# A whole first-stage order, row factors and pool scale by transposes, and 36 idle transposes at the start of TensorE

## Chip, cores and metric

One core of one Trainium2 chip runs the kernel. The metric is the device time of one execution in microseconds: 1158.05 us, the median of three runs (1158.02, 1158.05 and 1160.07). An instruction's place is given in us from the start of the profiled span.

## What is computed

Two layers over 512 latent rows and 256 context rows of 1024 channels. Layer 0 mixes by pooling, layer 1 by attention, and a squared-ReLU MLP follows each. The change touches the start of layer 0: row norm, conditioning vectors, the pooling mixer, and the first matmuls of its MLP. Cut to that:

```python
def modulate(h, shift, scale):
    return h * (1.0 + scale) + shift

def pool_mixer(h, w_pool, pool_scale):
    ...
        mean = (jnp.take(csg, hi, axis=1) - jnp.take(csg, lo, axis=1)) / cnt
        diff = (mean - hf[..., sl]).astype(h.dtype)
        outs.append(diff @ w_pool[g])
    return jnp.concatenate(outs, axis=-1) * pool_scale

def reference(...):
    for i in range(DEPTH):
        sh1, sc1, gt1, sh2, sc2, gt2 = ada_mods(c, w_ada[i], b_ada[i])
        csh1, csc1, cgt1, csh2, csc2, cgt2 = ada_mods(c_ctx, w_ada[i], b_ada[i])
        h_lat = modulate(rms_norm(x, g_mix_pre[i]), sh1, sc1)
        h_ctx = modulate(rms_norm(ctx, g_mix_pre[i]), csh1, csc1)
        ...
        x = x + gt1 * rms_norm(y_lat, g_mix_post[i])
        m_lat = sq_relu_mlp(modulate(rms_norm(x, g_mlp_pre[i]), sh2, sc2), w_mlp_in[i], w_mlp_out[i])
        x = x + gt2 * rms_norm(m_lat, g_mlp_post[i])
        ...
    return x
```

## The kernel before

Rows lie in six tiles of 128: t = 0 to 3 are latent, t = 4 and 5 context. The 1024 channels are eight blocks k of 128, two to each of the four pooling windows g. Large matmuls take operands split into a rounded half and a remainder (`hi` and `lo`), three products for one.

The first stage is written by hand. `FIRST` is one list of steps, and each step emits the instructions of one small piece of work. TensorE, VectorE and ScalarE keep the order in which the list emits their instructions (the wrapper `Kept`), and each executes them in that order; so a step that waits holds back all later steps of its engine, and no others. After the stage a scheduler places the instructions with a simulated timeline. Weight loads go through SyncE (SP) in program order, into seven raw buffers of 1 MB: four in `rawe`, three in `rawp`; `turns` says for each conditioning block which of the two pools it takes. A load is issued when its buffer is free.

The names of the steps:

- Row norm: `rows_a(t)` takes the mean square on ScalarE, adds epsilon on VectorE and takes the power on GpSimd; `rows_b(t)` (step `rb`) scales the row tile on VectorE into `acc`. Before the list, six `rows_a` and five `rows_b` stand at times of their own.
- Band: `band_mm(t, ks)` multiplies the scaled row tile by a band matrix (window mean minus identity), one fp32 matmul, which is two instructions, for each k; it writes `psm` (latent) or `psc` (context). `band_edge(v)` builds the bands of the first and the last tile from the loaded one. `ev` and `evc` move the sums to SBUF, on ScalarE where the step has a star, otherwise on VectorE.
- Conditioning: `mm:X_j` multiplies a loaded block of `w_ada` by the two conditioning vectors (the sums lie in 32-row groups), `rows` transposes it on VectorE, `sel` adds the groups by four small matmuls, `mods` adds the bias. SC1, SH1, GT1, SC2 and SH2 are the scale, shift and gate of the mixer and the scale and shift of the MLP. The blocks are loaded in the order SC1 and SH1 (0 to 3 in turn), GT1_0a, GT1_0b, GT1_2a, GT1_2b, `w_in`, SC2_0a, SC2_0b, SH2_0a, SH2_0b, SC2_2, SH2_2, SC2_3, SH2_3.
- Pooling: `wsc` multiplies the pool weights by `pool_scale`, which `pool_weights` spreads over the partitions by a matmul with one row; `wph` and `wpl` split them; `hi` and `lo` scale and split the band sums of a block k; `pool:t:g` makes six matmuls; `ms`, `rs` and `c` take its mean square, its factor and a copy.
- Gate and residual: `gc` makes gate columns, `psg` (`gate_half`) spreads four of them over the partitions by four fp32 matmuls against the identity, `gate` copies them to SBUF, `b` multiplies, `r` adds to `xr`.
- MLP input: `s`, `rs2` and `n` norm the new rows, `turn` transposes them (four transposes of 128x128), `h` modulates, `xhi` and `xlo` split, `in:t:q:f` makes six matmuls of the MLP; `whi` and `wlo` split its weights.

PSUM has two pools: `psA`, two buffers of two banks, and `psB`, four buffers of one bank. `psA` holds the latent band sums, the pool products of tiles 0, 2, 3 and 5 and the MLP sums; `psB` holds the rest.

Of the kernel before, what the change touches and what calls it, by code (L numbers as in the profile page):

```python
# [17 lines left out]
P = 128  # L18
# [13 lines left out]
HALO = 8  # L32
# [9 lines left out]
ev:0* ev:2 psc0:4 psm:4 rb:5 wsc:0 psm:6 wsc:1 ev:4* wph:0 mm:SC1_0 wph:1 wpl:0 mm:SH1_0 ev:6* rows:SC1_0 wpl:1  # L42
psc0:5 sel:SC1_0 rows:SH1_0 evc:2* mods:SC1_0 evc:0* sel:SH1_0 mm:SC1_1 mods:SH1_0 hi:0 psc:4 rows:SC1_1 hi:1
psc:6 lo:0 mm:SH1_1 evc:4* lo:1 evc:6* sel:SC1_1 rows:SH1_1 pool:4:0 mods:SC1_1 sel:SH1_1 mm:SC1_2 mods:SH1_1
hi:2 pool:0:0 rows:SC1_2 pool:5:0 hi:3 lo:2 mm:SH1_2 lo:3 sel:SC1_2 rows:SH1_2 pool:4:1 mods:SC1_2 sel:SH1_2
ms:4:0 mm:SC1_3 mods:SH1_2 hi:4 c:4:0 pool:5:1 rows:SC1_3 mm:SH1_3 hi:5 lo:4 sel:SC1_3 pool:0:1 rows:SH1_3
mods:SC1_3 sel:SH1_3 lo:5 pool:1:0 pool:1:1 mods:SH1_3 pool:5:2 hi:6 mm:GT1_0a ms:1:0 lo:6 pool:4:2 hi:7
mm:GT1_0b c:1:0 lo:7 pool:0:2 mm:GT1_2a rows:GT1_0 pool:4:3 sel:GT1_0 ms:4:1 mm:GT1_2b w_in mods:GT1_0 gc:0:0
gc:1:0 c:4:1* rs:4 pool:0:3 rows:GT1_2 psg:0:0 ms:0 sel:GT1_2 psg:1:0 c:0* mods:GT1_2 rs:0 gc:0:1 gc:1:1 psg:1:1
gate:1:0 gate:0:0 pool:5:3 b:4:0 gate:1:1 b:1:0 mm:SC2_0a ms:5 b:4:1 psg:0:1 r:4 c:5* rs:5 pool:1:2 gate:0:1 b:5  # L50
mm:SC2_0b s:4 pool:1:3 r:5 whi:0 rs2:4 pool:3:0 ms:1:1 rows:SC2_0 pool:3:1 c:1:1* b:0 mm:SH2_0a rs:1 n:4*
sel:SC2_0 b:1:1 mm:SH2_0b s:5 r:0 pool:2:0 whi:1 rs2:5 pool:2:1 rows:SH2_0 pool:2:2 s:0 mods:SC2_0 r:1 sel:SH2_0
mm:SC2_2 n:5* rs2:0 mods:SH2_0 wlo:0 pool:2:3 s:1 turn:4:0 n:0 turn:4:1 ms:2 rs2:1 mm:SH2_2 h:4:1 h:4:0* rs:2
pool:3:2 n:1 xhi:4:0 mm:SC2_3 rows:SH2_2 xhi:4:1 rows:SC2_2 xlo:4:0 sel:SH2_2 turn:0:1 xlo:4:1 sel:SC2_2 h:0:1*
pool:3:3 mods:SH2_2 mods:SC2_2 turn:0:0 b:2 xhi:0:1 mm:SH2_3 ms:3 xlo:0:1 in:4:0:1 h:0:0* rows:SH2_3 rs:3
in:4:1:1 b:3 xhi:0:0 in:0:1:1 r:3 turn:0:2 in:4:0:0 h:0:2* xlo:0:0 in:4:1:0 s:3 r:2 in:0:1:0 in:0:0:1 xhi:0:2
# [36 lines left out]
def backbone(ctx: ExitStack, tc, x, ctx_in, w_ada, w_pool, pool_scale, w_qkv, g_q, g_k, w_o, w_mlp_in,  # L93
# [134 lines left out]
    given = phase[:, 16:32]  # L228
    sy.dma_start(given, vecs[:, 160:176])
# [10 lines left out]
    one = sm_tile("sm")  # L240
    ve.memset(one, 1.0)
# [87 lines left out]
    def gate_half(ci, h):  # L329
        ps = psB.tile([P, 512], F32, tag="b", name="psg")  # L330
        gc = halfgate.pop((ci, h))
        for k in range(4):
            te.matmul(ps[:, k * P:(k + 1) * P], gc[:, 4 * h + k:4 * h + k + 1].broadcast_to([P, P]), ident,
                      start=True, stop=True)
        halfgate[ci, h] = ps
# [105 lines left out]
    def band_edge(v):  # L441
        c = (HALO, P)[v]
        ve.tensor_copy(bands[:, v], bands[:, 2])
        ve.tensor_copy(bands[:, v, :, c:c + HALO], edges[:, v])

    band_edge(0)

    means, lat, con = {}, {}, {}

    def band_open(k):  # L450
        lat[k] = psA.tile([P, 2, 512], F32, tag="a", name="psm")
        for u in range(2):
            means[k + u] = lat[k][:, u, :], None

    def band_open_c(k):
        con[k] = psB.tile([P, 2, 256], F32, tag="b", name="psc")
        for u in range(2):
            means[k + u] = means[k + u][0], con[k][:, u, :]

    def band_mm(t, ks):  # L460
# [4 lines left out]
        for k in ks:  # L465
            te.matmul(means[k][q][:, lo:hi], accv[:, t, k * P:(k + 1) * P], bands[:, v, k // 2, c0:c0 + hi - lo],
                      start=(i == 0 and (q == 0 or k % 2 == 0)), stop=(i == n - 1), skip_group_check=True)

    def band_ev(k, q, on_act):
        to = accv[:, (0, NL)[q]:(NL, NT)[q], P * k:P * k + 256]  # L470
        (sc.copy if on_act else ve.tensor_copy)(to, (lat, con)[q][k].rearrange("p u (a n) -> p (u a) n", n=256))
        for u in range(2):
            means[k + u] = (means[k + u][0], to[:, u, :]) if q else (to[:, 2 * u:2 * u + 2, :], means[k + u][1])
# [3 lines left out]
    def rows_a(t):  # L477
        ss, ms, rs[t] = sm_tile("ss"), sm_tile("ms"), sm_tile("rs")
        mean_square(xr[:, t, :], ss[:, 0:1])
        ve.tensor_scalar(out=ms[:, 0:1], in0=ss[:, 0:1], scalar1=EPS, scalar2=None, op0=ALU.add)  # L480
        gp.tensor_tensor(out=rs[t][:, 0:1], in0=ms[:, 0:1], in1=nhalf[:, 0:1], op=ALU.pow)

    def rows_b(t):
        scaled(accv[:, t, :], t, rs[t])
# [16 lines left out]
    pw = []  # L501
# [22 lines left out]
    def pool_a(t, g):  # L524
        if t not in mix:
            if t in (4, 1):
                mix[t] = [psB.tile([P, 512], F32, tag="b", name="pspool") for _ in range(2)]
            else:
                mix[t] = psA.tile([P, 2, 512], F32, tag="a", name="pspool")
# [251 lines left out]
    turns.extend((0, 0, 0, 0, 1, 1, 0, 0, 1, 0, 0, 1, 0, 0, 1, 0, 0, 1, 0, 0))  # L781
# [15 lines left out]
    st.at(14, pool_load)
# [33 lines left out]
    def keep(store, key, fn, *args):  # L831
# [3 lines left out]
        rb=rows_b, psc0=lambda t: band_mm(t, range(4)), psm=band_rows, psc=band_context,  # L835
# [23 lines left out]
    for n, what in enumerate(FIRST.split()):  # L859
        st.at(14.5 + n / 1000, step, what)  # L860
# [671 lines left out]
_INS = ["x", "ctx", "w_ada", "w_pool", "pool_scale", "w_qkv", "g_q", "g_k", "w_o", "w_mlp_in", "w_mlp_out"]  # L1532
_VECS = ["b_ada", "g_mix_pre", "g_mlp_pre", "g_mix_post", "g_mlp_post", "c", "c_ctx"]
# [78 lines left out]
```

## Time and profile before

| | |
|---|---|
| median of the three runs | 1158.05 us |
| time of the profiled execution | 1160.61 us |
| its span, first to last instruction | 1158.8 us |
| mean granted TensorE clock | 0.999 |
| TensorE busy with matmuls | 99% of the span |
| VectorE, ScalarE, GpSimd busy | 81%, 55%, 6% |
| DMA, mean over the span | 127 GB/s |

A row of the timeline gives start, duration, engine, line, operation, output and inputs, and the count of instructions merged in it; brackets hold the idle time before it and what ended that. A row of the chain of waits gives start, duration, what the time belonged to, and a count. Steps emitted through the wrapper all carry line L89, so they are told apart by tile names: `psm` and `psc` band sums, `psada` conditioning, `pspool` pooling, `psg` spread columns, `psx` transposes, `psin` MLP input.

### The profile page before, as it was taken

To read this page: it belongs to the slowest core of one execution; us is meant where nothing else is said; L and a number is where in the kernel's file an instruction comes from. 1 tells how busy PE (TensorE), PEld (TensorE's weight loads), DVE (VectorE), ACT (ScalarE), POOL (GpSimd) and SP (SyncE) were. 2 spreads that over 40 slices of the span, in tenths; PEclk is the share of its full clock that TensorE was granted. 3 is DMA by queue.
4 is the path that set the end of the run, shared out by engine and by line. 5 is a ranking of instruction groups with operands and counts; after the bars stand their busy time and mean duration, and the time that the engine had idled before them with its cause. 6 is when DMAs were issued, how large, how long until landed. Compare 5 with 4: busy or idle time off the path is not lost.

```text
span 1158.8 us, 16048 instructions
## 1 busy us (share of the span) xinstructions
PE 1142.9 (99%) x6220; PEld 992.7 (86%) x6220; DVE 932.9 (81%) x1522; ACT 632.8 (55%) x1076; POOL 69.7 (6%) x113
## 2 busy tenths in 40 slices
PE   7999999999999999999999999999999999999997
PEld 5789899898898988998888889998988888888886
DVE  4699588889988997996777699867687679778876
ACT  5687555555354534555675367753676436534523
POOL 1050000000000000000242200001100000000001
PEclk9999999999999999999999999999999999999999
DMA  9973222334344444343522102115244214313212
GB/s 374 419 282 140 73 103 107 130 139 143 112 146 146 145 146 145 109 146 109 182 74 73 37 1 74 37 74 186 105 141 150 77 69 146 109 40 142 109 32 114
DMA packets 25518, 147.34 MB, mean 127 GB/s; under 512 B 2785, under 2 KB 5345, under 8 KB 9698
## 3 DMA queue, kind: packets, MB, share of 16 engines
q1 hardware_dynamic: 25442, 146.32, 34.8%
q8 instruction: 49, 0.80, 0.3%
q14 instruction: 27, 0.22, 0.1%
HBM read 138.96 MB, written 7.34 MB: 126 GB/s over the span
## 4 chain that ended last, share of the span: by engine, by line
PE 91%; issue 2%; DVE 2%; ACT 2%; POOL 2%; DMA 1%; SPq 0%; POOLq 0%; DVEq 0%; ACTq 0%
PE pso L890 24%; PE psin L745 18%; PE psin L621 16%; PE pso L1001 12%; PE psy L1427 3%; PE po L1402 3%; PE pss L1361 3%; PE psq L1147 2%; PE pspt L1383 2%; PE pspool L89 2%; PE psada L89 2%; PE psin L89 2%; PE psm L89 1%; PE psx L89 1%; PE psg L89 1%
## 5 line engine op out<-in xcount | busy, mean ns | idle before, releaser
L890 PE MATMUL pso<-units,rb 128*128 128x512 f32 x1152 | 278.5, 392 | 0.0
L890 PEld LDWEIGHTS pso<-units,rb 128*128 128x128 f32 x1152 | 214.8, 188 | 41.2
L304 DVE SCALAR_TENSOR_TENSOR rows<-raw,cond,rows 128x256 f32<-128x256 f32 x280 | 127.5, 480 | 2.0
L904 DVE TENSOR_TENSOR acc<-acc,pso 128x512 f32<-128x512 f32 x126 | 84.0, 682 | 40.8 <-PE pso L890 40.7
L621 PE MATMUL psin<-ra,rb 128*128 128x512 f32 (+1 forms) x310 | 87.8, 360 | 0.0
L1001 PE MATMUL pso<-units,pairs 128*128 128x512 f32 x336 | 82.6, 389 | 0.0
L621 PE MATMUL psin<-ra 128*128 128x512 f32 (+1 forms) x256 | 76.5, 376 | 0.0
L1001 PEld LDWEIGHTS pso<-units,pairs 128*128 128x128 f32 x336 | 63.1, 188 | 13.1
L1005 DVE TENSOR_TENSOR acc<-acc,pso 128x512 f32<-128x512 f32 x72 | 48.7, 683 | 26.3 <-PE pso L1001 26.3
L212 POOL TENSOR_SCALAR ms<-ss 128x1 f32<-128x1 f32 x15 | 10.4, 691 | 969.6 <-ACT junk L199 924.1
L745 PE MATMUL psin<-ra,units 128*128 128x384 f32 x336 | 65.6, 337 | 0.4 <-ACT psin L757 0.4
L745 PE MATMUL psin<-sums,units 128*128 128x384 f32 x336 | 64.1, 337 | 0.0
L745 PEld LDWEIGHTS psin<-ra,units 128*128 128x128 f32 x336 | 59.7, 188 | 4.0 <-ACT psin L757 0.9
L621 PEld LDWEIGHTS psin<-ra,rb 128*128 128x128 f32 x310 | 55.6, 189 | 8.7
L745 PEld LDWEIGHTS psin<-sums,units 128*128 128x128 f32 x336 | 58.9, 188 | 1.6
L171 DVE TENSOR_TENSOR units<-raw,units 128x1024 fp32r<-128x1024 f32 (+2 forms) x49 | 55.2, 1152 | 4.9 <-ACT units L168 4.8
L621 PE MATMUL psin<-rb 128*128 128x512 f32 (+1 forms) x155 | 55.8, 361 | 0.6 <-DVE rb L1496 0.6
L168 ACT CAST units<-raw 128x1024 fp32r<-128x1024 f32 (+2 forms) x49 | 46.8, 995 | 16.9 <-PE pso L890 12.8
L621 PEld LDWEIGHTS psin<-ra 128*128 128x128 f32 x256 | 47.1, 188 | 8.8
L902 ACT COPY acc<-pso 128x512 f32<-128x512 f32 x48 | 27.2, 588 | 48.7 <-PE pso L890 48.4
L1147 PE MATMUL psq<-units,ra 128*128 128x512 f32 x216 | 52.2, 393 | 0.0
L621 PE MATMUL psin<-rb,ra 128*128 128x512 f32 (+1 forms) x128 | 48.1, 376 | 0.0
(292 smaller groups left out, 2395.0 us busy)
## 6 DMA issues: line engine op xcount, KB each, us to landing
raw<-in_w_ada SPq DMA_DIRECT2D x48, 1024.0 KB, 5.1
raw<-in_w_mlp_in SPq DMA_DIRECT2D x32, 1024.0 KB, 4.9
raw<-in_w_mlp_out SPq DMA_DIRECT2D x32, 1024.0 KB, 5.0
raw<-in_w_qkv SPq DMA_DIRECT2D x6, 1024.0 KB, 5.0
spill<-xr SPq DMA_DIRECT2D x10, 512.0 KB, 5.5
xr<-spill SPq DMA_DIRECT2D x10, 512.0 KB, 7.0
raw<-in_w_o SPq DMA_DIRECT2D x4, 1024.0 KB, 4.9
xr<-in_x SPq DMA_DIRECT2D x4, 512.0 KB, 6.5
```

The source lines that it names most:

```text
L89: return lambda *args, **kw: self.tc.keep_in_program_order(f(*args, **kw))
L168: a = sc.copy(hi, raw)
L171: b = ve.tensor_tensor(out=lo, in0=raw, in1=hi, op=ALU.subtract)
L304: ve.scalar_tensor_tensor(out=r, in0=raw[:, k, :], scalar=cond[:, k, c:c + 1], in1=r, op0=ALU.mult, op1=ALU.add)
L621: te.matmul(ps[:, bank, o:o + ln], w[:, k, fs], rhs, start=start, stop=(k == KT - 1 and n == 2), skip_group_check=len(ks) < KT or self.paired)
L745: te.matmul(bank, w[k], a[k], start=start and k == 0 and m == 0, stop=stop and k == 3 and m == 2, skip_group_check=True)
L890: te.matmul(pss[h][:, 0:cols[h][1]], a[:, f, ts_], w[:, f, cols[h][0]:sum(cols[h])], start=(n == 0 and not seeded[t]), stop=(n == len(seq) ...
L904: ve.tensor_tensor(out=d, in0=d, in1=ps[:, 0:w], op=ALU.add)
L1001: te.matmul(ps, a, w, start=(m == 0), stop=(m == len(seq) - 1))
L1005: ve.tensor_tensor(out=M[n][:, t], in0=M[n][:, t], in1=ps, op=ALU.add)
L1147: te.matmul(ps, a[:, k, sl], w[:, k % 4, :], start=(k == 0 and n == 0), stop=(k == KT - 1 and n == 2))
L1361: te.matmul(ps[:, c2, 0:384], a[:, sl], b[:, kv, 384 * c2:384 * c2 + 384], start=(n == 0), stop=(n == 2))
```

## The change

The steps of the row norm, the band edges and all band matmuls become entries of `FIRST`, which starts at time 1 and holds the whole stage in a new order. The stars say where an evacuation, a norm or a modulation runs.

```diff
 FIRST = """
-ev:0* ev:2 psc0:4 psm:4 rb:5 wsc:0 psm:6 wsc:1 ev:4* wph:0 mm:SC1_0 wph:1 wpl:0 mm:SH1_0 ev:6* rows:SC1_0 wpl:1
-psc0:5 sel:SC1_0 rows:SH1_0 evc:2* mods:SC1_0 evc:0* sel:SH1_0 mm:SC1_1 mods:SH1_0 hi:0 psc:4 rows:SC1_1 hi:1
...
-rs2:3 wlo:1 s:2 in:0:0:0 turn:0:3 xlo:0:2 n:3* sel:SH2_3 rs2:2 turn:4:2 rows:SC2_3 in:0:2:0 mods:SH2_3 h:4:2*
...
+xs:0 xe:0 xp:0 xn:0 xs:1 xe:1 xs:2 edge:0 xp:1 psm:0:2 xn:1 xs:3 psm:0:0 xe:2 psm:0:4 xp:2 psm:1:2 xs:4 xn:2
+psm:1:4 psm:0:6 xe:3 xp:3 edge:1* psm:2:4 xe:4 psm:2:2 xp:4 xn:3 xs:5 psm:1:0 psm:3:4 psm:3:2 ev:4* xe:5 psm:2:0
+xp:5 xn:4* psm:3:0 pw:0 ev:5* psm:1:6 wsc:0 psm:2:6 psm:3:6 pw:1 ev:7* ev:6 wph:0 wsc:1 mm:SC1_0 ev:0* psc:4:0
+rows:SC1_0 xn:5 mm:SH1_0 wph:1 sel:SC1_0 ev:2* rows:SH1_0 psc:5:0 mods:SC1_0 psc:4:2 evc:0 sel:SH1_0 psc:5:2
+mods:SH1_0 mm:SC1_1 wpl:0 hi:0 psc:4:6 rows:SC1_1 evc:2* psc:5:6 lo:0 hi:1 mm:SH1_1 sel:SC1_1 evc:6* psc:4:4
+mods:SC1_1 psc:5:4 rows:SH1_1 lo:1 sel:SH1_1 evc:4* mm:SC1_2 mods:SH1_1 pool:0:0 rows:SC1_2 hi:2 wpl:1 pool:5:0
+hi:3 sel:SC1_2 mm:SH1_2 lo:2 pool:1:0 mods:SC1_2 rows:SH1_2 sel:SH1_2 mm:SC1_3 mods:SH1_2 lo:3 hi:4 pool:4:0
+pool:1:1 lo:4 mm:SH1_3 ms:1:0 rows:SC1_3 hi:5 pool:4:1 rows:SH1_3 c:1:0 sel:SC1_3 sel:SH1_3 pool:5:1 mods:SH1_3
+mods:SC1_3 pool:0:1 lo:5 hi:7 mm:GT1_0a hi:6 lo:7 pool:0:2 mm:GT1_0b ms:4:0 lo:6 pool:5:2 rows:GT1_0 pool:0:3
+c:4:0 sel:GT1_0 ms:0 mm:GT1_2a mods:GT1_0 gc:1:0 gc:0:0 psg:0:0 rs:0 c:0 pool:1:2 gate:0:0 mm:GT1_2b w_in
+psg:1:0 rows:GT1_2 pool:1:3 gate:1:0 b:1:0 sel:GT1_2 pool:2:0 whi:0 mods:GT1_2 gc:0:1 gc:1:1 b:4:0 psg:0:1
+ms:1:1 pool:5:3 wlo:0 gate:0:1 pool:4:2 rs:1 c:1:1* b:0 pool:4:3 ms:5 psg:1:1 b:1:1 pool:2:1 ms:4:1 rs:5 r:0
+mm:SC2_0a c:4:1* gate:1:1 rs:4 mm:SC2_0b r:1 c:5* pool:2:2 s:0 b:4:1 pool:3:0 r:4 s:1 pool:3:1 rs2:0 pool:3:2
+rows:SC2_0 s:4 rs2:1 pool:2:3 b:5 n:0* mm:SH2_0a rs2:4 n:1 mm:SH2_0b ms:2 r:5 sel:SC2_0 n:4* turn:0:1 rows:SH2_0
...
+xhi:4:0 mm:SH2_3 h:4:2* xlo:4:0 in:0:1:1 whi:1 rows:SH2_3 in:4:1:0 r:3 s:2 in:4:0:1 sel:SH2_3 in:4:0:0 s:3
...
+in:2:2:1 h:2:0* xlo:2:1 in:2:2:0 xhi:2:0 in:2:3:0 xlo:2:0 in:2:1:0 in:2:0:1 in:2:0:0 in:2:3:1 in:4:3:1 in:2:1:1
 """
```

The steps behind the new names: `xs`, `xe`, `xp` and `xn` are the three parts of `rows_a` and `rows_b`, with `xn` on ScalarE under a star; `psm:t:k` and `psc:t:k` are `band_mm` for one row tile and two blocks; the sums of blocks 4 to 7 go to four `psB` buffers in place of two `psA` buffers.

```diff
+    def awake(n):
+        ps = psB.tile([P, 512], F32, tag="b", name="idle")
+        for k in range(n):
+            te.transpose(ps[:, (k % 4) * P:(k % 4 + 1) * P], ident, ident)
...
-    turns.extend((0, 0, 0, 0, 1, 1, 0, 0, 1, 0, 0, 1, 0, 0, 1, 0, 0, 1, 0, 0))
+    turns.extend((0, 0, 0, 0, 1, 1, 0, 0, 0, 0, 1, 1, 0, 0, 0, 0, 1, 1, 0, 0))
...
-    st.at(0.1, pool_weights, 0)
...
-    st.at(14, pool_load)
+    st.at(0.05, awake, 36)
+    st.at(0.5, pool_load)
```

`pool_scale` is no longer loaded as a row; it comes with the vectors, as eight columns, and is spread by transposes, and so are the gate columns:

```diff
-    given = phase[:, 16:32]
-    sy.dma_start(given, vecs[:, 160:176])
+    given, pool_cols = phase[:, 16:32], phase[:, 32:40]
+    sy.dma_start(phase[:, 16:40], vecs[:, 160:184])
...
     xload(0)
-    scale_row = work_tile()[0:1]
-    sy.dma_start(scale_row, pool_scale[0:1])
+    xload(1)
     sy.dma_start(gate.rearrange("p a n -> p (a n)")[:, 8 * BW:12 * BW + 64], band)
-    for t in range(1, NT):
+    for t in range(2, NT):
         xload(t)
...
         for k in range(4):
-            te.matmul(ps[:, k * P:(k + 1) * P], gc[:, 4 * h + k:4 * h + k + 1].broadcast_to([P, P]), ident,
-                      start=True, stop=True)
+            te.transpose(ps[:, k * P:(k + 1) * P], gc[:, 4 * h + k:4 * h + k + 1].broadcast_to([P, P]), ident)
...
     def pool_weights(h):
         ps = psB.tile([P, 512], F32, tag="b", name="psg")
-        te.matmul(ps, one[0:1, 0:1].broadcast_to([1, P]), scale_row[:, 512 * h:512 * h + 512], start=True, stop=True)
-        pw.append(ps)
+        for k in range(4):
+            te.transpose(ps[:, k * P:(k + 1) * P], pool_cols[:, 4 * h + k:4 * h + k + 1].broadcast_to([P, P]), ident)
+        pooled_scale[h] = ps
```

The pool products of tiles 4 and 1 take their second `psB` buffer when the second half begins, where before they took both at once. `gate_half` is also called twice in layer 1.

More of the change, by code (lines that the diff above doesn't have):

```diff
@@ L47 @@
[L47 to L56, printed above, removed]
@@ new lines @@
+ms:1:1 pool:5:3 wlo:0 gate:0:1 pool:4:2 rs:1 c:1:1* b:0 pool:4:3 ms:5 psg:1:1 b:1:1 pool:2:1 ms:4:1 rs:5 r:0
+mm:SC2_0a c:4:1* gate:1:1 rs:4 mm:SC2_0b r:1 c:5* pool:2:2 s:0 b:4:1 pool:3:0 r:4 s:1 pool:3:1 rs2:0 pool:3:2
+rows:SC2_0 s:4 rs2:1 pool:2:3 b:5 n:0* mm:SH2_0a rs2:4 n:1 mm:SH2_0b ms:2 r:5 sel:SC2_0 n:4* turn:0:1 rows:SH2_0
+mm:SC2_2 s:5 mods:SC2_0 sel:SH2_0 rows:SC2_2 pool:3:3 mods:SH2_0 rs2:5 b:2 h:0:1* turn:0:0 sel:SC2_2 mm:SH2_2
+h:0:0* n:5 mods:SC2_2 turn:4:0 xhi:0:0 rows:SH2_2 turn:4:1 ms:3 xlo:0:0 sel:SH2_2 mm:SC2_3 mods:SH2_2 xhi:0:1
@@ new lines @@
+rs:3 b:3 in:0:0:0 h:4:1* turn:4:2 rs:2 xlo:0:1 xhi:4:1 in:0:0:1 rows:SC2_3 h:4:0* in:0:1:0 xlo:4:1 r:2 sel:SC2_3
+xhi:4:0 mm:SH2_3 h:4:2* xlo:4:0 in:0:1:1 whi:1 rows:SH2_3 in:4:1:0 r:3 s:2 in:4:0:1 sel:SH2_3 in:4:0:0 s:3
+mods:SH2_3 rs2:2 mods:SC2_3 wlo:1 turn:0:2 xhi:4:2 turn:4:3 rs2:3 in:4:1:1 h:4:3* xlo:4:2 turn:0:3 n:2 h:0:2*
+in:4:2:0 n:3 in:4:2:1 xhi:4:3 turn:2:3 xhi:0:2 xlo:4:3 turn:2:1 h:0:3* turn:2:2 xlo:0:2 in:4:3:0 h:2:1 xhi:0:3
+in:0:2:1 h:2:2* xlo:0:3 in:0:2:0 h:2:3 xhi:2:2 in:0:3:1 xlo:2:2 in:0:3:0 xhi:2:3 xhi:2:1 turn:2:0 xlo:2:3
@@ L92, in backbone @@
 @with_exitstack
[L93 removed]
+def backbone(ctx: ExitStack, tc, x, ctx_in, w_ada, w_pool, w_qkv, g_q, g_k, w_o, w_mlp_in,
              w_mlp_out, vecs, rope, band, out):
@@ L439, in backbone, with band_edge @@
     edges = gflat[:, 12 * BW:12 * BW + 64].rearrange("p (v g n) -> p v g n", v=2, g=4)
[L441 to L448, printed above, removed]
+    def band_edge(v, on_act):
+        c, copy = (HALO, P)[v], sc.copy if on_act else ve.tensor_copy
+        copy(bands[:, v], bands[:, 2])
+        copy(bands[:, v, :, c:c + HALO], edges[:, v])
+    means, lat, con = {k: [None, None] for k in range(KT)}, {}, {}
     def band_open(k):
-        lat[k] = psA.tile([P, 2, 512], F32, tag="a", name="psm")
+        if k < 4:
+            lat[k] = psA.tile([P, 2, 512], F32, tag="a", name="psm")
         for u in range(2):
-            means[k + u] = lat[k][:, u, :], None
+            if k >= 4:
+                lat[k + u] = psB.tile([P, 512], F32, tag="b", name="psm")
+            means[k + u][0] = lat[k][:, u, :] if k < 4 else lat[k + u]
     def band_open_c(k):
@@ L464, in band_mm @@
         c0 = lo - (i * P - HALO)
-        for k in ks:
+        if i == 0:
+            (band_open, band_open_c)[q](k0)
+        for k in (k0, k0 + 1):
             te.matmul(means[k][q][:, lo:hi], accv[:, t, k * P:(k + 1) * P], bands[:, v, k // 2, c0:c0 + hi - lo],
@@ L469, in band_ev, with row_square, row_eps, row_pow @@
     def band_ev(k, q, on_act):
[L470 to L473, printed above, removed]
-    rs, mix, yg, copied, first = {}, {}, {}, {}, []
[L477 to L484, printed above, removed]
+        n = P if q == 0 and k >= 4 else 256
+        to = accv[:, (0, NL)[q]:(NL, NT)[q], P * k:P * k + n]
+        src = (lat, con)[q][k]
+        src = src.rearrange("p (a n) -> p a n", n=n) if n == P else src.rearrange("p u (a n) -> p (u a) n", n=n)
+        (sc.copy if on_act else ve.tensor_copy)(to, src)
+        for u in range(n // P):
+            means[k + u][q] = to if n == P else to[:, u, :] if q else to[:, 2 * u:2 * u + 2, :]
+    rs, mix, yg, copied, first = {}, {}, {}, {}, []
+    def row_square(t):
+        rs[t] = sm_tile("ss")
+        mean_square(xr[:, t, :], rs[t][:, 0:1])
+    def row_eps(t):
+        ms = sm_tile("ms")
+        ve.tensor_scalar(out=ms[:, 0:1], in0=rs[t][:, 0:1], scalar1=EPS, scalar2=None, op0=ALU.add)
+        rs[t] = ms
+    def row_pow(t):
+        r = sm_tile("rs")
+        gp.tensor_tensor(out=r[:, 0:1], in0=rs[t][:, 0:1], in1=nhalf[:, 0:1], op=ALU.pow)
+        rs[t] = r
+    def row_scaled(t, on_act):
+        if on_act:
+            sc.activation(accv[:, t, :], xr[:, t, :], AF.Copy, scale=rs[t][:, 0:1])
+        else:
+            scaled(accv[:, t, :], t, rs[t])
     def centred(k, part):
@@ L489, in centred @@
             if ci == 0:
-                hi, lo = (z.rearrange("p (a n) -> p a n", n=256) for z in (hi, lo))
+                hi, lo = (z.rearrange("p (a n) -> p a n", n=256 if k < 4 else P) for z in (hi, lo))
             sa = avec[0][0][:, k, ci:ci + 1]
@@ L524, in pool_a @@
     def pool_a(t, g):
[L525 to L529, printed above, removed]
+        if t in (4, 1):
+            if g % 2 == 0:
+                mix.setdefault(t, {})[g // 2] = psB.tile([P, 512], F32, tag="b", name="pspool")
+        elif t not in mix:
+            mix[t] = psA.tile([P, 2, 512], F32, tag="a", name="pspool")
         to, sl = mix[t][g // 2] if t in (4, 1) else mix[t][:, g // 2, :], slice(t * P, (t + 1) * P)
@@ L834, in backbone @@
     kinds = dict(
-        rb=rows_b, psc0=lambda t: band_mm(t, range(4)), psm=band_rows, psc=band_context,
+        xs=row_square, xe=row_eps, xp=row_pow, xn=row_scaled, edge=band_edge, psm=band_mm, psc=band_mm, pw=pool_weights,
         ev=lambda k, act: band_ev(k, 0, act), evc=lambda k, act: band_ev(k, 1, act),
@@ L854, in step @@
         args = [int(a) if a.isdigit() else a for a in args]
-        if kind in ("c", "n", "h", "ev", "evc"):
+        if kind in ("c", "n", "h", "ev", "evc", "edge", "xn"):
             args.insert(1, what[-1] == "*")
@@ L859, in backbone @@
     for n, what in enumerate(FIRST.split()):
-        st.at(14.5 + n / 1000, step, what)
+        st.at(1 + n / 1000, step, what)
     st.at(100, ordered.__setitem__, 0, False)
```

40 lines of the change are left out of this document (6 added, 34 removed).

## The prediction

> **What bounds the kernel now.** I read the page first, then who waited for whom on TensorE, then the chain of waits and the timeline of the first 100 us, then the landings of the loads.
>
> ```profile
> span 1158.8 us, 16048 instructions
> PE 1142.9 (99%) x6220; PEld 992.7 (86%) x6220; DVE 932.9 (81%) x1522; ACT 632.8 (55%) x1076; POOL 69.7 (6%) x113
> ...
> PE psg L89 <- DMA work<-in_pool_scale: 5.1, 1, 5.1
> PE psm L89 <- DVE acc L89: 2.0, 2, 1.1
> ...
> PE psin L621 <- DVE rb L1496: 0.6, 1, 0.6
> PE psg L89 <- DVE gc L89: 0.3, 1, 0.3
> ```
>
> TensorE is the bound nearly everywhere. It waits in the first 12 us; after that its longest wait is 0.6 us, and the first stage holds one of 0.3. So after the stage a microsecond saved early comes through whole, and inside it the time is TensorE's own work and its pace. The chain shows both:
>
> ```profile
> 11.36 2.29 PE psm L89 x8
> 13.65 2.00 PE psg L89 x2
> 15.65 3.80 PE psm L89 x16
> 19.45 0.93 PE psc L89 x8
> 20.38 1.92 PE psm L89 x16
> ...
> 46.69 0.91 PE pspool L89 x6
> 47.60 1.00 PE psada L89 x8
> ...
> 50.56 0.91 PE pspool L89 x6
> 51.47 0.89 PE psg L89 x8
> 52.36 0.18 PE psada L89 x8
> 52.54 1.10 PE psg L89 x8
> ...
> 53.97 1.13 PE psg L89 x8
> ...
> 56.80 1.09 PE psg L89 x8
> ...
> 84.50 1.75 PE psx L89 x16
> ...
> 88.11 8.63 PE psin L89 x72
> 96.74 16.64 PE psin L621 x96
> ```
>
> The same band matmuls take 3.80/16 = 237 ns each from 15.65 and 1.92/16 = 120 ns from 20.38: the array runs at half pace until about 19.3 us, though the profile's granted clock is 0.999 overall. The stage ends at 96.74, where the next helper's matmuls begin. The last conditioning block of the gates, GT1_2b, ends on TensorE at 50.56, where the `pspool` row follows it, so 46.2 us (96.74 - 50.56) of dense work come after. What the loads allow is read from issue and time to landing of the first and twelfth `w_ada` load, and of the last (SH2_3):
>
> ```profile
> 5.87 0.43 SPq L149 DMA_DIRECT2D raw<-in_w_ada  x1
> raw<-in_w_ada SPq DMA_DIRECT2D x1, 1024.0 KB, 12.9
> ...
> 33.84 0.33 SPq L149 DMA_DIRECT2D raw<-in_w_ada  x1
> raw<-in_w_ada SPq DMA_DIRECT2D x1, 1024.0 KB, 13.3
> ...
> 59.66 0.33 SPq L149 DMA_DIRECT2D raw<-in_w_ada  x1
> raw<-in_w_ada SPq DMA_DIRECT2D x1, 1024.0 KB, 9.9
> ...
> 5.00:10.00 5.00, 3.98 (x10) 2.35 (x10) 1.61 (x5) 2.47 (x5) 0.59 (x2) 1.00 1.00 405
> 60.00:70.00 10.00, 10.00 (x114) 6.96 (x112) 9.31 (x14) 9.68 (x17) 9.11 (x11) 1.00 1.01 416
> ```
>
> SC1_0 lands at 18.8, GT1_2b at 47.1 and SH2_3 at 69.6, from 5 to 70 us with the DMA engines full (share 1.00 and 1.01, the last but one figure), about one block in 2.5 us. TensorE before is 50.56 - 1.0 - 47.1 = 2.4 us late for GT1_2b: that is all that a better order can win up to there, since no order makes the block land sooner.
>
> **The change, part by part.** Start. The first tile's path and the bands:
>
> ```profile
> 5.02 1.06 ACT L89 ACTIVATE junk<-xr 128x1024 bf16<-128x1024 f32 x1 [0.91 <-DMA xr<-in_x]
> 5.84 0.46 DVE L443 COPY gate<-gate 128x576 f32<-128x576 f32 x1 [4.07 <-DMA gate<-in_band]
> 7.25 0.75 DVE L89 TENSOR_SCALAR acc<-xr,rs 128x1024 f32<-128x1024 f32 x1 [0.68 <-POOL rs L481]
> 1.00 0.29 POOL masks.py:199 TENSOR_SCALAR_AFFINE_SELECT ident<-ident 128x128 f32<-128x128 f32 x1
> ```
>
> The scaled tile is ready at 8.0. The band now stands behind one more row tile, 512 KB at 405 GB/s or 1.3 us, so it lands near 7.1, and its edge copy, with an epsilon step ahead of it on VectorE, ends between 7.8 and 8.8. I let the first band matmul start at 8.8, against 8.06 before. Sixteen band steps of four instructions take 16 x 0.48 = 7.7 us at the fast pace, and the two `pw` 8 x 0.109 = 0.9 (1.75/16 = 109 ns a transpose): 17.4, if the row tiles come as fast as before. SC1_0 is there at 18.8, so TensorE has 1.4 us to spare, and a start later by that much is free.
>
> Idle transposes. The identity is ready at 1.3 us. 36 transposes take 3.9 us at 109 ns and 7.9 at twice that, so they end between 5.2 and 9.2, beside a wait that before lasted till 8.06. Cost: nothing, or 0.4 us of delay at 8.8, which is inside the spare 1.4. If the spare is gone, 0.4. Their tile takes a `psB` buffer that nothing reads, so TensorE's own order frees it. Their gain is that the sixteen steps run at the fast pace. No row before has transposes on a slow array; from below the gain is nothing (a rival below), from above the whole slow stretch.
>
> From SC1_0's landing to GT1_2b the new list holds eleven `mm` (11.0), eight `psc` steps (8 x 0.5 = 4.0, by 0.93 for two), nine `sel` (1.6), twelve `pool` (10.9) and one `psg` (four transposes, 0.44): 27.9 us. 18.8 + 27.9 = 46.7, and the block lands at 47.1. TensorE now follows the loads step by step; with small waits I take 47.3 as its start and 48.3 as its end. Gain here: 50.56 - 48.3 = 2.3 us (between 1.0 if waits add 1.3, and 2.5).
>
> After GT1_2b the remaining pieces are those of before in another order (twelve `pool`, seven `sel`, eight `mm`, twelve `turn`, 24 `in`), except for the gate columns: four groups took 0.89 + 1.10 + 1.13 + 1.09 = 4.2 us with what they waited for; three groups of transposes take 3 x 0.44 = 1.3. Gain 2.9 (1.4 if only the instructions count: 3 x 0.45). End of stage: 48.3 + 46.2 - 2.9 = 91.6, 5.1 us sooner. SH2_3 is then met 1.0 + 21 x 0.72 + 7 x 0.44 + 0.2 = 19.4 before the end (21 `in`, seven `turn`, one `sel` stand behind it), at 72.2; it landed at 69.6, so the last load is no bound.
>
> VectorE and ScalarE:
>
> ```profile
> 53.66:92.01 38.35, 38.04 (x380) 31.31 (x381) 34.32 (x55) 34.34 (x60) 16.49 (x20) 1.00 0.77 309
> 53.66 1.07 ACT L89 COPY gate<-psg 128x512 f32<-128x512 f32 x2
> ```
>
> From the first gate copy to the last split both were busy 34.3 of 38.4 us. The new list makes its first gate, 0:0, ahead of GT1_2b, near 47; six `in` stand behind the last split, so that must end by 91.6 - 4.3 = 87.3: 40 us for the same 34.3 of work. The stars move one 1024-wide copy and one norm from ScalarE to VectorE and two `h` back; a copy is 1.0 to 1.2 us, a norm 0.75 or 1.15, an `h` 1.0, so each engine's total stays within 0.1 us. Enough room on the whole, but at the end ScalarE's steps from `h:4:1` to the last split sum to about 16.4 us with hardly a gap. For waits that this makes I take 0.8 us off the gain (from none to 5: its neighbour is the 0.3 us that is the old stage's only one after 20 us).
>
> Loads. The pool-scale row goes, so later issues move up by one slot of about 0.4 us, landings by 0 to 0.4; I count none. The `turns` change which buffer a block waits for; loads are issued 10 to 13 us ahead of landing, a transfer takes 2.5, so a buffer freed 7 us later still costs nothing. The epsilon, power and memset steps are those of before or fewer.
>
> Layer 1 calls `gate_half` twice:
>
> ```profile
> 769.33 0.22 PE psg L333 x2
> 770.62 1.56 PE psg L333 x14
> ```
>
> 1.78 us become 8 x 0.109 = 0.87: gain 0.9, TensorE being dense there.
>
> Sum: -2.3 - 2.9 + 0.8 - 0.9 = -5.3 us. The profiled execution took 1160.61 us with 1158.8 of span, so 1155.3 by its own; it stands 2.6 above the median, as one of the three runs does (1160.07), and against the median the sum is 1158.05 - 5.3 = **1152.8 us**.
>
> **Rivals.** (1) The transposes don't wake the array. For: the array before became fast 3.4 us after 15.65, where full matmuls began to follow each other, and no row shows transposes doing it. Against: nothing either way. Then they end at 9.2, band steps take 0.95 us, and the array wakes 3.4 to 6.8 us later, after 4 to 7 steps: 2 to 3.3 us lost, of which 1.0 is spare (1.4 less the 0.4 of delay) and about 0.4 more is waiting for GT1_2b: 0.6 to 1.9 of loss. 1154.0. The Trainium skill, TensorE: Matmul & The Clock Gate, Part 4, says that transposes don't count as TensorE activity for the clock gate; by that rule this rival is the forecast, and no trace here shows it yet.
>
> (2) The tail is bound by the order on ScalarE and VectorE. For: both 89% busy there before, and each holds back all behind a late step. Against: the order before made TensorE wait 0.3 us in all. If each of the eight chains of `turn`, `h`, `xhi`, `xlo` for the last two pairs waits a 0.5 us step, 4 us are lost: 1156.8.
>
> (3) Slower: the array falls back to half pace while TensorE waits for loads between 18.8 and 47. For: before, waits of 0.9 and 1.1 us among matmuls went with the slow pace up to 19.3. Against: after 0.6 us of wait no slowing shows, and the waits worked out above are about 1.4 and less. Price: every us of fast work takes 2. It decides from 7.6 us of such work (5.3 to give back and 2.3 beyond); at 11 of the 27.9, the end is 1158.05 - 5.3 + 11 = 1163.8. The same page, Part 1, puts the fall at an idle window of some 3.4 us, which would speak against it.
>
> **How the numbers follow.** Chances: forecast 0.52, rival (1) 0.18, (2) 0.14, (3) 0.12, other slower ends 0.04. A measurement of this kernel can't tell less than 0.2%, 2.3 us, from no change. Faster holds most of the first two and a third of (2): 0.72; slower is (3) and the rest: 0.16; the same 0.12. The forecast's own range is 1150.0 to 1155.5, from no waits and landings 0.4 sooner, with 1.5 for later stages that the scheduler places anew, to waits of 3. The range over the cases goes up through (2) to 1159.5, which leaves the slower cases out, and starts at 1149.8.
>
> **What would show it.** In the changed profile: `psm` instructions of about 120 ns from the first on (else rival 1); TensorE waiting for `w_ada` loads between 18 and 47, and GT1_2b's matmuls ending by 48 to 49; `psg` groups of 0.44 us; line L621 starting near 92; nothing but `psg` different behind it. The forecast is wrong if L621 starts after 94.5, if matmuls after 20 us take twice their time, or if TensorE's waits for VectorE and ScalarE in the stage exceed 3 us.

## The result and the profile after

The changed kernel takes 1155.64 us (median of 7 runs, 1155.01 to 1156.29) against 1160.07 us of the kernel before (7 runs, 1158.02 to 1162.18, the three shown earlier among them). The ratio is 0.9958, 95% interval 0.9948 to 0.9967: faster by 4.4 us in the medians. The forecast was 5.3 us less, 1152.8 counted from a median of 1158.05; with more runs that median is about 2 us higher, and the experiments bear on why its runs spread. The profiled execution of the changed kernel took 1156.15 us, 0.5 above its median.

The waits of TensorE in the changed kernel's first 100 us (instruction, what it waited for: us in total, times, longest):

```profile
PE psada L91 <- DMA raw<-in_w_ada: 1.8, 1, 1.8
...
PE psm L91 <- DVE gate L91: 1.2, 1, 1.2
PE psx L91 <- DVE acc L91: 0.5, 1, 0.5
PE psada L91 <- DVE mods L91: 0.3, 1, 0.3
PE psx L91 <- ACT acc L91: 0.3, 1, 0.3
...
```

It waits for one conditioning block, 1.8 us; the rows left out are the 1.3 us until the identity is ready and 0.2 us for a row tile. In what follows the array is called awake where TensorE works at the fast pace, about 120 ns for a band matmul instruction, and asleep where it takes about twice that. Rows of TensorE's timeline (start, duration), with layer 1's gate columns at the end:

```profile
1.34 5.82 PE L91 MATMUL idle<-ident 128*128 128x128 f32 x36 [1.34 <-POOL ident masks.py:199]
8.37 4.78 PE L91 MATMUL psm<-gate,acc 128*128 128x136 f32 x36 [1.20 <-DVE gate L91]
...
17.69 1.07 PE L91 MATMUL psada<-raw,cond 128*32 128x256 f32 x16
...
21.24 1.37 PE L91 MATMUL psada<-raw,cond 128*32 128x256 f32 x16 [1.82 <-DMA raw<-in_w_ada]
...
22.60 2.18 PE L91 MATMUL psc<-gate,acc 128*128 128x136 f32 x8
...
26.75 1.19 PE L91 MATMUL psc<-gate,acc 128*128 128x136 f32 x8
...
48.03 1.07 PE L91 MATMUL psada<-raw,cond 128*32 128x512 f32 x8
49.03 0.65 PE L91 MATMUL psg<-ident,gc 128*128 128x128 f32 x4
...
765.52 0.27 PE L332 MATMUL psg<-ident,gc 128*128 128x128 f32 x1
...
767.38 3.00 PE L1427 MATMUL psy<-ra 128*128 128x512 f32 x12
```

And the row of its chain of waits in which the next helper, L637, begins:

```profile
93.21 16.64 PE psin L637 x96
```

The stage ends at 93.21 instead of 96.74, 3.5 us sooner. GT1_2b's matmuls end at 49.1 (50.56 before): 1.5 us of that is won by there, and the remaining 2.1 behind it (44.1 us of work instead of 46.2). In layer 1 the stretch from the first gate column to line L1427 lasts 1.9 us instead of 2.8 (769.17 to 771.94): 0.9. Together 4.4, which is the difference of the two spans, 1158.8 and 1154.4. Behind that nothing is left over to explain. GT1_2b landed at 32.87 + 13.6 = 46.5 and TensorE came to it at 48.03, 1.5 us later and without a wait, so here its own work, and not this load, set when the gates were ready.

One stretch is worse than it should be. Eight `psc` instructions take 2.18 us at 22.60 and 1.19 at 26.75. Busy time, count and granted clock of TensorE in three stretches (the third figure from the end of a row is the clock; DMA share and GB/s follow):

```profile
21.30:24.60 3.30, 3.30 (x32) 0.59 0.97 405
24.60:25.30 0.70, 0.70 (x10) 0.51 1.16 480
25.40:40.00 14.60, 14.60 (x204) 1.00 1.01 419
```

After the 1.8 us wait for the second conditioning block, SH1_0, the array was asleep for about 3.4 us: a clock of 0.59 over 3.3 us is 2.7 us at one half, and 0.7 us follow.

### The profile page after: what moved, and what is told of

Same layout as the page of the kernel before. It is cut to its first block, busy times and chain, and to the rows that moved or that the text cites. A ratio compares the mean times of both kernels' runs of the same rounds, so it can differ in the third digit from the quotient of the medians.

```text
span 1154.4 us, 16072 instructions
## 1 busy us (share of the span) xinstructions
PE 1140.3 (99%) x6236; PEld 992.9 (86%) x6236; DVE 930.9 (81%) x1517; ACT 632.5 (55%) x1082; POOL 70.5 (6%) x113
## 4 chain that ended last, share of the span: by engine, by line
PE 89%; issue 3%; POOL 3%; DVE 2%; DMA 2%; ACT 2%; SPq 0%; POOLq 0%; DVEq 0%; ACTq 0%
PE pso L890 24%; PE psin L761 18%; PE psin L637 16%; PE pso L1001 12%; PE psy L1427 3%; PE po L1402 3%; PE pss L1361 3%; PE psq L1147 2%; PE pspt L1383 2%; PE psin L91 2%; PE psada L91 1%; DMA raw<-in_w_ada 1%; POOL rs L216 1%; PE pspool L91 1%; POOL rs L1156 1%
## 5 line engine op out<-in xcount | busy, mean ns | idle before, releaser
L637 PE MATMUL psin<-ra,rb 128*128 128x512 f32 (+1 forms) x310 | 87.8, 360 | 0.0
L637 PE MATMUL psin<-ra 128*128 128x512 f32 (+1 forms) x256 | 76.5, 376 | 0.0
L1001 PEld LDWEIGHTS pso<-units,pairs 128*128 128x128 f32 x336 | 63.1, 188 | 13.1
L637 PEld LDWEIGHTS psin<-ra,rb 128*128 128x128 f32 x310 | 55.6, 189 | 8.7
L637 PE MATMUL psin<-rb 128*128 128x512 f32 (+1 forms) x155 | 55.9, 362 | 0.6 <-DVE rb L1496 0.6
L637 PEld LDWEIGHTS psin<-ra 128*128 128x128 f32 x256 | 47.1, 188 | 8.7
L637 PE MATMUL psin<-rb,ra 128*128 128x512 f32 (+1 forms) x128 | 48.1, 376 | 0.0
```

The lines of the kernel that those rows point to most:

```text
L637: te.matmul(ps[:, bank, o:o + ln], w[:, k, fs], rhs, start=start, stop=(k == KT - 1 and n == 2), skip_group_check=len(ks) < KT or self.paired)
L1001: te.matmul(ps, a, w, start=(m == 0), stop=(m == len(seq) - 1))
```

## The experiments

Each kernel is the one before or the changed one with one thing altered; the stage end is where the chain of waits enters the next helper.

**Without the idle transposes.**

```diff
-    st.at(0.05, awake, 36)
```

> The changed kernel without its 36 idle transposes. Theory (the loads set the pace up to GT1_2b, so a slow start is mostly absorbed): the first band matmul stays near 8.4 us, runs at about 230 ns an instruction for 3.4 to 6.8 us, the block SC1_0 is met at 19.5 to 21 us instead of 17.7, GT1_2b ends 0.4 to 1.9 us later than 49.1, the stage ends at 93.8 to 95.1 instead of 93.2, and the time is 0.6 to 1.9 us above the changed kernel's 1155.6. Rival (the idle transposes carry the whole gain): the stage ends near 96.7 and the time is that of before, about 1160. Rival (they carry nothing): stage end 93.2, same time.

1155.59 us (4 runs, 1155.54 to 1155.78), the changed kernel's time, and a stage end of 92.61 in the chain, 0.6 sooner than in the changed kernel's profiled execution, as that execution's own time is 0.6 longer. From its timeline:

```profile
8.36 7.83 PE L91 MATMUL psm<-gate,acc 128*128 128x136 f32 x52 [8.36 <-DVE gate L91]
...
18.43 1.07 PE L91 MATMUL psada<-raw,cond 128*32 128x256 f32 x16
...
20.13 1.07 PE L91 MATMUL psada<-raw,cond 128*32 128x256 f32 x16
...
28.58 1.07 PE L91 MATMUL psada<-raw,cond 128*32 128x256 f32 x16 [0.92 <-DMA raw<-in_w_ada]
...
46.83 1.07 PE L91 MATMUL psada<-raw,cond 128*32 128x512 f32 x8
```

The end of its stage in the chain:

```profile
92.61 16.64 PE psin L637 x96
```

The band matmuls did start at the slow pace, and the first block was met 0.7 us later; but SH1_0 lands earlier here and the wait for it is gone, so GT1_2b ends at 47.9, 1.2 us sooner than with the transposes. It landed at 31.34 + 14.6 = 45.9 and was met at 46.83, 0.9 us later. "They carry nothing" holds, and not only because the loads absorb a slow start. The transfers tell the rest: one instruction fetch (queue, packets, MB, share of the 16 engines in that microsecond) stands in the window 17 to 18 us of the changed kernel:

```profile
q8 instruction: 1, 0.02, 6.6%
```

and in the window 24 to 25 us of this one:

```profile
q8 instruction: 1, 0.02, 6.7%
```

Around each the landing of one block comes about 1 us late. SC1_0 lands at 6.18 + 11.4 = 17.6 in the changed kernel and SH1_0, issued at 6.97, 14.1 later, at 21.1: 3.5 us apart where blocks come in 2.5. With 72 instructions more ahead on TensorE (36 weight loads, 36 transposes), the first fetch comes 7 us sooner and falls on the block that TensorE wants next. The other traces agree on the move: the first fetch comes at 17.3 to 21.0 in the four kernels with 36 idle transposes, at 21.4 with 18, and at 23.7 to 28.8 in the seven executions without. On the late block they agree in part. In eight of the twelve profiled executions the next block to land after the first fetch has ended comes 3.4 to 3.8 us behind the one before it; in three of the old order, with the first fetch at 27.7 to 28.8, that block is not late. So a fetch alone is not enough to delay a block, and that it is the cause where one is late was not tried apart.

**Gate columns by matmuls again.**

```diff
-            te.transpose(ps[:, k * P:(k + 1) * P], gc[:, 4 * h + k:4 * h + k + 1].broadcast_to([P, P]), ident)
+            te.matmul(ps[:, k * P:(k + 1) * P], gc[:, 4 * h + k:4 * h + k + 1].broadcast_to([P, P]), ident,
+                      start=True, stop=True)
```

> The changed kernel with the gate columns spread by fp32 matmuls again, two instructions where one transpose stands. Theory: each of four groups takes 0.45 us more, the stage ends 1.8 us later (95.0), layer 1 loses 0.9 more, time +2.7 us (1158.3). Rival (the waits around them come back too, as the 4.2 us of before count them): stage +2.9, time +3.8. Rival (TensorE's work there is hidden behind loads or behind VectorE and ScalarE): stage +0 to 0.5, time +0.9 to 1.4.

1158.05 us (10 runs): 2.4 above the changed kernel. The end of its stage in the chain:

```profile
94.56 16.64 PE psin L638 x96
```

That is 1.35 later, and layer 1 loses its 0.9. The theory's 2.7 is close; of the 1.8 us of TensorE's instructions 1.35 reach the stage end. What the change spreads by transposes are these gate columns and the pool scale; the row factors, which the title names, are taken on VectorE and GpSimd as before (`xe`, `xp`).

**Idle transposes alone, on the kernel before**, with the helper `awake` of the change.

```diff
+    st.at(0.05, awake, 36)
     st.at(0.1, pool_weights, 0)
```

> The kernel before with nothing added but the 36 idle transposes at its start. Theory: its band matmuls run at about 120 ns from 8 us on, the first conditioning block is met some 3 us sooner, but GT1_2b lands at 47.1 and was met at 49.5, so the stage gains at most 2.4 us, ending near 94.3, and the time falls by about 2.4. Rival (no load binds, the whole slow stretch comes back): stage end 93.2 or less, time down 3.5. Rival (the array is slow again by the time of the band matmuls): nothing.

1158.17 us (10 runs, 1157.53 to 1160.05); ratio to before 0.998, interval 0.997 to 0.999, 2.4 us less in the medians. The array is awake 3 us after the transposes begin. TensorE now waits for conditioning blocks, 1.0 us in three places; GT1_2b's matmuls start at 47.22, 0.4 us after its landing at 30.62 + 16.2 = 46.8. The end of the stage in the chain:

```profile
94.47 16.64 PE psin L621 x96
```

The theory had 94.3: the loads cap what an awake array buys in the old order.

**Gate columns by transposes alone, on the kernel before**, the reverse of the diff of the gate columns above.

> The kernel before with its gate columns spread by transposes. Theory: four groups of 0.44 us in place of 0.89 to 1.13, the stage ends 1.8 to 2.9 us sooner (93.8 to 94.9), layer 1 gains 0.9, time down 2.7 to 3.8 us. Rival (the columns were waiting for VectorE and ScalarE, so shorter work only waits longer): stage under 0.8 us sooner, time down 0.9 to 1.7.

1158.13 us (9 runs, 1155.92 to 1159.38); ratio 0.9979, interval 0.9969 to 0.999, 2.5 us less. The runs spread over 3.5 us, and the profiled execution was the fastest of them. So the same program, and the kernel before, were profiled once more.

> The kernel before with the gate columns by transposes once more, for a second profile of the same program: its first profiled execution took 1155.9 us, its median was 1158.1. Theory (the spread of the old order is the moment at which the array becomes fast, 11.4 us in that execution and 19.0 in the profiled one of before): an execution near 1158 shows the slow pace of 230 ns an instruction until 18 to 20 us, one near 1156 only until 11 to 13. Rival (the spread has another source): no such pairing.

> The kernel before once more, for a second profile: its profiled execution took 1160.6 us and its array became fast at 19.0 us; its times run from 1158.0 to 1162. Theory: near 1158.0 the array becomes fast by 11 to 13 us, near 1160.5 at 18 to 20, later still above 1161. Rival (the spread has another source): no such pairing.

The times were 1158.95 and 1161.46. The band matmuls, first in the execution of 1155.92 with transposed gate columns:

```profile
13.06 2.17 PE L89 MATMUL psm<-gate,acc 128*128 128x144 f32 x16
...
15.37 1.19 PE L89 MATMUL psc<-gate,acc 128*128 128x136 f32 x8
```

in that of 1158.95, the same program:

```profile
15.51 4.10 PE L89 MATMUL psm<-gate,acc 128*128 128x144 f32 x16
...
19.40 1.93 PE L89 MATMUL psc<-gate,acc 128*128 128x136 f32 x8
...
21.17 3.98 PE L89 MATMUL psm<-gate,acc 128*128 128x136 f32 x32
```

and in the kernel before at 1161.46 (that of 1160.61 stands in the prediction):

```profile
15.65 4.10 PE L89 MATMUL psm<-gate,acc 128*128 128x144 f32 x16
...
19.54 1.75 PE L89 MATMUL psc<-gate,acc 128*128 128x136 f32 x8
...
21.13 3.98 PE L89 MATMUL psm<-gate,acc 128*128 128x136 f32 x32
```

Sixteen `psm` in 2.17 us are fast, in 4.10 slow; eight `psc` in 1.19 are fast, in 1.75 to 1.93 slow. So the array was awake before 13.1 in the execution of 1155.92, between 19 and 19.5 in that of 1160.61, and only about 21 in the two others. In these executions, two of each program, the pairing is as the theory has it: where the array wakes later the time is longer (with transposed columns the stage ends at 92.94 and 95.86, in the kernel before at 96.74 and 97.64). No execution of the kernel before near 1158 was profiled, so that the whole of its spread is the moment of waking is not shown.

**The order alone**: the changed kernel with both edits, no idle transposes and gate columns by matmuls. The pool scale by transposes stays in it; no run takes that apart.

> The changed kernel without its idle transposes and with the gate columns by matmuls again: what is left is the new order and the pool scale by transposes. Theory (idle transposes worth nothing in this order, gate columns 2.4 us): 1158.0 us, stage end 94 to 94.6, with the few tenths of spread that the kernel without idle transposes had. Rival (the idle transposes only looked worthless because the faster gate columns hid it): 1159 or more. Rival (the order itself gains nothing): that of before, 1160.6.

1157.32 us (8 runs, 1157.01 to 1157.52), 3.4 below the 1160.77 of the kernel before, measured beside it, ratio 0.9973, interval 0.9962 to 0.9983. Against the kernel without idle transposes the gate columns are worth 1.7 us here, not 2.4. The end of the stage in the chain:

```profile
93.29 16.64 PE psin L638 x96
```

With transposed columns it is 92.61, so only 0.7 of their 1.8 us reach the stage end. GT1_2b's matmuls end at 48.5, 2.1 us sooner than in the kernel before, though nothing wakes the array ahead of its work: the band matmuls follow each other without a pause and are fast from about 11.8 on.

**The old order with both**: idle transposes and transposed gate columns added to the kernel before.

> The kernel before with the idle transposes and the gate columns by transposes, in its old order. Theory (a new order and an awake array buy the same 2.4 us, up to the landing of GT1_2b, and the gate columns add theirs): 1160.6 - 2.4 - 2.4 = 1155.8, stage end 92.6 to 93.2, as in the changed kernel. Rival (the new order has a gain of its own behind GT1_2b): 1156.6 or more.

1156.60 us (5 runs, 1155.54 to 1156.68); ratio 0.9962, interval 0.9948 to 0.9977. That overlaps the changed kernel's 1155.01 to 1156.29, so a share of the new order's own, under 1 us, stays open; the rival set its mark at 1156.6, where the median lies. Its profiled execution took 1156.6 us, and there the array fell asleep again. Before, in and after that stretch (length; busy time and count of TensorE, its weight loads, VectorE, ScalarE and GpSimd; clock, DMA share, GB/s):

```profile
6.90:13.70 6.80, 5.98 (x34) 3.94 (x33) 3.08 (x8) 4.82 (x9) 1.63 (x4) 1.00 1.02 409
13.80:17.00 3.20, 3.20 (x15) 3.20 (x15) 1.63 (x4) 1.46 (x3) 1.16 (x3) 0.50 1.03 433
17.20:24.00 6.80, 6.80 (x75) 5.74 (x74) 6.05 (x7) 4.00 (x5) 0.00 (x0) 1.00 1.01 418
```

**Eighteen idle transposes**: `36` becomes `18`.

> The changed kernel with 18 idle transposes in place of 36. They end near 5.1 us, after 3.8 us of work; the first band matmul comes at 8.4, after 3.2 us of nothing. Theory (an awake array stays awake over a wait of some us): if the transposes reach the fast pace, the band matmuls start at 120 ns an instruction. Rival (it falls asleep): they start at 230 ns. Either way about 1155.6 us, since the loads absorb it.

1155.43 us in a single execution, within the changed kernel's range. They end at 5.4, still at the slow pace, and TensorE then waits 2.9 us. The stretch in which the band matmuls begin, in the same columns without GpSimd:

```profile
8.40:9.00 0.60, 0.60 (x5) 0.60 (x6) 0.44 (x1) 0.47 (x1) 0.99 1.04 423
9.20:12.40 3.20, 3.20 (x15) 3.20 (x15) 1.20 (x6) 2.92 (x7) 0.50 1.06 428
12.50:16.00 3.50, 3.50 (x32) 3.50 (x31) 0.77 (x2) 2.69 (x6) 1.00 1.02 426
```

They start fast (5 in 0.6 us), fall to half clock after 0.6 us, stay there 3.4 us, and rise. Both readings were partly wrong: the array woke, and fell asleep a little after work had begun again.

**The epsilon step on VectorE**, without the idle transposes. In the changed kernel GpSimd adds epsilon and takes the power of every row factor behind the first row norm:

```profile
51.93 2.09 POOL L214 TENSOR_SCALAR ms<-ss 128x1 f32<-128x1 f32 x1 [4.01 <-ACT junk L91]
54.11 0.85 POOL L216 TENSOR_TENSOR rs<-ms,nhalf 128x1 f32<-128x1 f32 x1
...
63.14 1.46 POOL L216 TENSOR_TENSOR rs<-ms,nhalf 128x1 f32<-128x1 f32 x1
```

One column takes up to 2.1 us there, and from 51.9 to 64.6 one such step follows the other.

```diff
         ms, r = sm_tile("ms"), sm_tile("rs")
+        add = ve if mixed[0] else gp
         if parts == 1:
-            gp.tensor_scalar(out=ms[:, 0:1], in0=ss[:, 0:1], scalar1=EPS, scalar2=None, op0=ALU.add)
+            add.tensor_scalar(out=ms[:, 0:1], in0=ss[:, 0:1], scalar1=EPS, scalar2=None, op0=ALU.add)
...
-            gp.tensor_scalar(out=ms[:, 0:1], in0=ss[:, parts - 1:parts], scalar1=rest, scalar2=EPS,
+            add.tensor_scalar(out=ms[:, 0:1], in0=ss[:, parts - 1:parts], scalar1=rest, scalar2=EPS,
```

> The changed kernel without its idle transposes, and with the epsilon step of every row factor of the first stage on VectorE in place of GpSimd, where it took up to 2.1 us for one column. Theory (the waits of TensorE behind GT1_2b, 1.8 us in three places, end with a row factor from GpSimd's queue): the waits fall under 0.6, the stage ends 1 to 1.5 us sooner, 91.1 to 91.6, time 1154.1 to 1154.6. Rival (VectorE now waits in its own order for mean squares of ScalarE): no gain, or up to 1 us slower.

1153.74 us (4 runs, 1153.65 to 1154.05); ratio to before 0.9944, interval 0.9929 to 0.9959. This beats both kernels: 1.85 us below the one without idle transposes. TensorE's waits in its first 100 us are three:

```profile
PE psm L91 <- DVE gate L91: 8.3, 1, 8.3
PE psada L91 <- DMA raw<-in_w_ada: 0.4, 1, 0.4
PE psada L91 <- DVE mods L91: 0.2, 1, 0.2
```

The waits for row tiles (`psx`), 1.5 us without the idle transposes, are gone. GT1_2b's matmuls end at 48.0, as in the kernel without idle transposes (47.9), so the gain lies wholly behind them. The moved step in VectorE's timeline, and the end of the stage in the chain:

```profile
53.47 0.15 DVE L91 TENSOR_SCALAR ms<-ss 128x1 f32<-128x1 f32 x1
```

```profile
90.67 16.64 PE psin L638 x96
```

The step takes 0.15 us on VectorE, and the stage ends 1.9 us sooner than 92.61, a little more than forecast; the 1.5 us of waits account for most of it. In the kernel without idle transposes the chain runs through GpSimd alone from 50.7 to 64.0, and once more at 66.3:

```profile
50.74 2.10 POOL ms L214
...
52.91 0.85 POOL rs L216
...
66.62 0.58 POOL rs L216
```

The waits of the changed kernel named VectorE and ScalarE as what `psx` waited for; these had themselves been waiting for GpSimd's two steps (behind 47 us VectorE 2.9 us, ScalarE 1.6).

## Why the prediction was right, and where its sizes were off

**The path to GT1_2b.** The gain was 1.5 instead of 2.3 us, 49.1 against the forecast 48.3, and inside its 1.0 to 2.5. Two steps failed. "TensorE now follows the loads step by step" did not come: it waited for one block, SH1_0, and from there its own work set the pace, so GT1_2b was met 1.5 us after its landing. And "with small waits I take 47.3": that one wait was 1.8 us, and the half clock behind it doubled the work of the next 3.4. Without the idle transposes GT1_2b ended at 47.9, a gain of 2.7 and a little beyond the range, with one wait of 0.9 and no half clock. The landings moved up by more than the 0 to 0.4 allowed, too: SC1_0 from 18.8 to 17.6, GT1_2b from 47.1 to 46.5.

**Why the order gains.** The forecast gave the whole order no price apart from the transposes. Alone it was worth 3.4 us, and what it wins up to GT1_2b looks like an earlier waking. In the old order GT1_2b's matmuls end at 50.56 to 51.50 where the array woke at 19 to 21 us, but at 47.98 in the execution of 1155.92 that woke before 13, and at 48.27 with idle transposes; the new order ends them at 47.9 to 49.7. So an old order awake early is as soon there as the new one. This is read from traces, not tried: no run gave the new order its pauses back.

**The idle transposes.** "Cost: nothing" was right to 0.1 us in the time, but for the wrong reason: the cost was priced as delay at 8.8, which there was none of (first band matmul at 8.4), and no price was set on the instructions themselves, with which the wait for SH1_0 and the half clock came. Rival (1), that transposes don't wake the array, is refuted. Counts and clock of the idle transposes of the changed kernel:

```profile
1.60:4.60 3.00, 3.00 (x15) 3.00 (x15) 1.00 0.82 235
4.92:6.90 1.98, 1.98 (x21) 1.98 (x19) 1.00 1.05 391
```

A new transpose starts every 213 ns in the first stretch and every 109 in the second (the counts take in those that reach over the stretch's ends), with nothing but transposes on TensorE: the step came 3.5 us after their start. The rule of the Trainium skill, TensorE: Matmul & The Clock Gate, Part 4, that transposes don't count as activity for the clock gate, does not hold here. What the forecast missed is that the new order doesn't need them: with them or without, 1155.6.

**The gate columns.** "Gain 2.9, or 1.4 if only the instructions count": with the allowance of 0.8 for waits the net behind GT1_2b was 2.1 forecast and 2.1 measured, but it is made up otherwise. With columns by matmuls the new order has 44.9 us behind GT1_2b (94.56 less 49.68), so 1.3 of the 2.1 come from the order, which has one of the four groups ahead of GT1_2b, and 0.8 from the transposes. At the stage end the experiments put 1.35 us on the columns in the changed kernel and 0.7 without idle transposes; with the shorter columns TensorE's waits behind GT1_2b grow there from 0.8 to 1.1 and from 0.8 to 1.8 us, and so swallow saved work. In layer 1, 0.9 as forecast.

**VectorE and ScalarE.** 0.8 us of waits were allowed; TensorE waited 1.1 in three places behind GT1_2b, so the 4 us of rival (2) did not come. The place was not foreseen. The prediction called the epsilon and power steps "those of before or fewer" and gave GpSimd no part in any sum. Moving one of its two steps away was worth 1.9.

**Rival (3), sleep while waiting for loads**, happened, over about 3.4 us instead of the 7.6 from which it would have decided, and cost part of the 1.2 us by which GT1_2b was later than without idle transposes. The argument against it, that after waits of 0.6 us no slowing shows, was drawn from shorter waits than the one that came. The Trainium skill, TensorE: Matmul & The Clock Gate, Part 1, puts the fall at an idle window of some 3.4 us. Here 1.8 us of wait were enough, so the measurement differs.

**The level.** The sum was set against 1158.05. The old order's runs depend, as far as the four profiles show, on when the array wakes, and that median of three was a fast one; by the medians of 7 the difference was 4.4 of the forecast 5.3. The measured 1155.64 lies inside the range over the cases, 1149.8 to 1159.5, and 0.1 above the forecast's own, 1150.0 to 1155.5, which by its own terms (waits of 3 in place of 0.8) ends at 1155.0; for 1149.8 no working is given. Rivals (1) and (2), at 1154.0 and 1156.8, lie nearer to it than the forecast's 1152.8 (1154.8 if counted from the median of seven), so the time alone does not choose between them; the traces do.

## What to carry to other kernels

Parts of a change that free the same resource don't add up: idle transposes alone gave 2.4 us, transposed columns 2.5 and the order 3.4, and all together 4.4. The idle transposes and the order both bring TensorE sooner to the same loads, so in the new order the transposes add nothing; the columns stand for the most part behind those loads and still added 1.7 to 2.4 there. Ask of an engine with 6% busy time whether it stands in series with the critical one: here two steps on single columns on GpSimd stood behind waits that named VectorE and ScalarE, and moving one of them won 1.9 us. And an order that lets TensorE start with dense full matmuls, with loads to wait for behind them, made the slow start nearly free and the times narrow here (1155.54 to 1155.78 in four runs, against 1158.02 to 1162.18 before).

## What the runs showed of the hardware

After dense work begins, the array woke within 2.6 to 5.6 us, at a moment that differs between kernels: after 3.5 us of transposes in the changed kernel, after 2.6 to 2.9 of band matmuls without them, and after about 5.5 of transposes in the old order with both edits. Where the first matmuls of the old order stood apart it was not awake before 19 to 21 us in three executions, and by 13 in a fourth, of a program that in another execution took until 21. In four profiled executions it fell to half clock for some 3.4 us, 0.6 us or more after work had resumed behind a wait: after 1.8 us (the changed kernel, and the one with columns by matmuls), after 2.9, and in the old order with both edits after 0.8 with one-row matmuls around it. It did not fall after the 0.9 us in the kernel without idle transposes, nor after 1.2 us in the old order with idle transposes alone, where one-row matmuls stand around the wait as well. So the length of the wait alone does not decide; what does stays open. The granted clock reads 0.50 in such a fall, but 1.00 in the first slow stretch of each execution, where only the pace of the instructions shows it (15 transposes in 3.0 us against 21 in 2.0).
